# Rotary embedding on half of each head: the first load in two pieces, and one store on another queue

## The chip, the cores and the metric

The kernel runs on one core of one Trainium2 chip. The metric is the device time of one execution in microseconds (us). Runs are repeated, and the median is given with the lowest and the highest. One execution is also taken by the hardware profiler; the profile's times count from the start of its span, which is a little shorter than the time of the execution.

The engines that matter here are VectorE (DVE in the profile), which does all the arithmetic, GpSimd (POOL) and SyncE (SP), which issue transfers, and the core's 16 DMA engines, which carry them. SP's transfers run on the queue that the profile calls q1 (hardware_dynamic), POOL's on q0 (software_dynamic). A trailing q, as in SPq, means an engine's sequencer.

## The reference

```python
batch, seq, heads, dim = (16, 512, 16, 64)          # x is float32
x1, x2 = x[..., :32], x[..., 32:]
cos, sin = cos[None, :, None, :], sin[None, :, None, :]   # given as (512, 32)
first  = x1[..., :16] * cos[..., :16] - x1[..., 16:] * sin[..., :16]
second = x1[..., :16] * sin[..., :16] + x1[..., 16:] * cos[..., :16]
out = concatenate([first, second, x2], axis=-1)
```

The first 32 of each head's 64 numbers are rotated, the other 32 are copied. Only the first 16 columns of cos and sin are used. The input is 33.55 MB and the output as much.

## The kernel before

The input is cut into four tiles (T = 4). A tile has 128 partitions with 16 rows (K) of 1024 floats each, so 64 KB of contiguous memory on each partition and 8.39 MB in all. Half of every row is not changed; the kernel loads it with the rest and stores it from the same place. The tiles live in `ring`, which has three slots (NS = 3), so tile 3 takes the slot of tile 0.

Before the first tile is turned, cos and sin are fetched by GpSimd's queue (lines 63 and 64) into `stage`, after VectorE has cleared it (line 61). VectorE spreads them over the partitions into `table` (lines 73 to 86). Then `rotate(t, lo, hi)` turns the rows lo to hi of a tile in four VectorE instructions: the product with sin goes to the PSUM tile `b_t` (line 96), the product with cos stays in place (line 97), and a subtraction and an addition finish the two halves (lines 98 and 101). A tile is turned in two halves of eight rows (KC = 8), and then stored whole: that is `turn(t)` (line 105).

All loads of x and all stores are issued by SP, in the order in which they are written, and SP waits at each for what it needs. The order is:

- load 0, load 1, the first half of load 2 (lines 65 to 67), which need no wait;
- store 0 (from `turn(0)`), which waits for the rotation of tile 0;
- the second half of load 2 (line 111);
- load 3 in 14 and 2 rows (lines 112 and 113, KL = 14), which needs the slot of tile 0 and so waits for store 0 to land;
- store 1 (line 116), with a wait added by hand (line 115): it is not issued before the first piece of load 3 has landed;
- store 2 and store 3 (lines 121 and 122), each after the rotation of its tile.

The end of the program (line 148 in the profile) waits for all transfers. `load` and `store` are the two helpers at lines 54 and 57, so that all loads have line 55 in the profile, and all stores line 58.

Of the kernel before, what the change touches and what calls it, by code (L numbers as in the profile page):

```python
# [1 line left out]

# [4 lines left out]


@with_exitstack
def kernel(  # L10
    ctx: ExitStack,
    tc: tile.TileContext,
    x: bass.AP,
    cos: bass.AP,
    sin: bass.AP,
    out: bass.AP,
):
    nc = tc.nc
    fp32 = mybir.dt.float32
    P = 128  # L20
    B, S, H, D = x.shape
    Q = D // 4
    HF = D // 2

    K = 16
    T = B * S // (P * K)
    PB = S // K
    REP = P // PB  # L30
    R = H * D
    NS = 3
    KC = K // 2
    KL = 14

    xf = x.rearrange("b s h d -> (b s h d)").rearrange("(t p f) -> t p f", t=T, p=P)
    of = out.rearrange("b s h d -> (b s h d)").rearrange("(t p f) -> t p f", t=T, p=P)
    cosf = cos.rearrange("(p k) j -> p (k j)", k=K)
    sinf = sin.rearrange("(p k) j -> p (k j)", k=K)

    const_pool = ctx.enter_context(tc.tile_pool(name="const", bufs=1))
    b_pool = ctx.enter_context(tc.tile_pool(name="bp", bufs=1, space=bass.MemoryType.PSUM))


    ring = const_pool.tile([P, NS, K, H, D], fp32)
    stage = const_pool.tile([P, 2, K, HF], fp32)
    spun = const_pool.tile([P, 2 * K, Q], fp32)
    packed = const_pool.tile([PB, 2 * K, Q], fp32)
    table = const_pool.tile([P, 2, K, 2, Q], fp32)

    def rows(t, lo, hi):
        return ring[:, t % NS, lo:hi].rearrange("p k h d -> p (k h d)")

    def load(t, lo=0, hi=K):
        return nc.sync.dma_start(out=rows(t, lo, hi), in_=xf[t, :, lo * R : hi * R])

    def store(t, lo=0, hi=K):
        return nc.sync.dma_start(out=of[t, :, lo * R : hi * R], in_=rows(t, lo, hi))


    nc.vector.memset(stage[:, :, :, 0:Q], 0.0)  # L61
    spread = stage.rearrange("(j b) t k i -> j b t (k i)", b=REP)
    nc.gpsimd.dma_start(out=spread[:, 0, 0], in_=cosf)  # L63
    nc.gpsimd.dma_start(out=spread[:, 0, 1], in_=sinf)  # L64
    load(0)
    load(1)
    load(2, 0, KC)

    PQ = PB // REP
    nc.vector.stream_shuffle(  # L73
        out=spun[:],
        in_=stage.rearrange("p t k j -> p (t k) j")[:, :, 0:Q],
        mask=[j % PQ * REP for j in range(PB)],
    )
    for q in reversed(range(REP)):
        n = PQ * (q + 1)
        nc.vector.tensor_copy(out=packed[0:n], in_=spun[q * PB : q * PB + n])  # L80

    for r in range(REP):
        nc.vector.tensor_copy(  # L83
            out=table[r * PB : (r + 1) * PB].rearrange("p t k c j -> p (t k) c j"),
            in_=packed.unsqueeze(2).to_broadcast((PB, 2 * K, 2, Q)),
        )
    C = table[:, 0].rearrange("p k c j -> p k (c j)")
    Sn = table[:, 1].rearrange("p k c j -> p k (c j)")

    def rotate(t, lo, hi):  # L90
        x1 = ring[:, t % NS, lo:hi, :, 0:HF]
        c = C[:, lo:hi].unsqueeze(2).to_broadcast((P, hi - lo, H, HF))
        s = Sn[:, lo:hi].unsqueeze(2).to_broadcast((P, hi - lo, H, HF))
        b_full = b_pool.tile([P, KC, H, HF], fp32, name="b_t")
        b_t = b_full[:, 0 : hi - lo]
        nc.vector.tensor_mul(out=b_t, in0=x1, in1=s)  # L96
        nc.vector.tensor_mul(out=x1, in0=x1, in1=c)  # L97
        nc.vector.tensor_sub(  # L98
            out=x1[:, :, :, 0:Q], in0=x1[:, :, :, 0:Q], in1=b_t[:, :, :, Q:HF]
        )  # L100
        nc.vector.tensor_add(  # L101
            out=x1[:, :, :, Q:HF], in0=x1[:, :, :, Q:HF], in1=b_t[:, :, :, 0:Q]
        )

    def turn(t):
        rotate(t, 0, KC)
        rotate(t, KC, K)
        return store(t)

    turn(0)  # L110
    load(2, KC, K)
    near = load(3, 0, KL)
    load(3, KL, K)

    tc.add_manual_dep(
        turn(1).ins,
        near.ins.name,
        mybir.DependencyInfo(mybir.DependencyClass.Sync, mybir.DependencyReason.DATA),
        reason="the store follows the loads at the DMA engines",
    )  # L120
    turn(2)
    turn(3)


# [1 line left out]
_INS = ['x', 'cos', 'sin']  # L126
_OUTS = [((16, 512, 16, 64), 'float32')]


# [23 lines left out]
```

## Time and profile before

| | us |
|---|---|
| time, median of 4 runs | 161.54 (161.49 to 161.84) |
| time of the profiled execution | 161.56 |
| its span | 159.8 |

The transfers, from their issues and the times to landing in the trace:

| transfer | queue | issued at, us | landed at, us |
|---|---|---|---|
| load 0 (16 rows) | SP | 0.74 | 23.00 |
| load 1 | SP | 1.17 | 42.35 |
| load 2, rows 0 to 8 | SP | 1.64 | 52.07 |
| cos, sin | POOL | 1.70, 2.35 | 10.77, 15.76 |
| store 0 | SP | 49.98 | 71.70 |
| load 2, rows 8 to 16 | SP | 50.37 | 81.42 |
| load 3, rows 0 to 14 | SP | 71.72 | 98.36 |
| load 3, rows 14 to 16 | SP | 72.09 | 100.84 |
| store 1 | SP | 98.43 | 120.16 |
| store 2 | SP | 103.77 | 139.45 |
| store 3 | SP | 130.66 | 158.74 |

VectorE's instructions, by line: eight of each, one per half tile.

| line | tile written <- read | mean, us | first and last start, us |
|---|---|---|---|
| 96 | b_t <- ring, table | 4.433 | 23.1 and 117.2 |
| 97 | ring <- ring, table | 4.424 | 27.6 and 121.7 |
| 98 | ring <- ring, b_t | 2.287 | 32.0 and 126.1 |
| 101 | ring <- ring, b_t | 2.280 | 34.2 and 128.4 |

The first table is read as three views of one time: the median is what counts, the profiled execution is one run, and the span is what its profile covers. In the second table the time between an issue and its landing holds the wait behind earlier transfers on the same queue, so the distance between two landings tells more of a transfer's cost than its own two numbers do. In the profile, a line `SPq L58 <- DVE ring L101` means that SP's sequencer stood before a store (line 58) until VectorE's addition (line 101) was done; the numbers are us in total, times, and the longest. A line of the DMA part gives packets, MB and the share of the time of 16 engines.

### The profile page before, as it was taken

What the parts mean: (1) busy time and instruction counts of PE and PEld (TensorE: products, weight loads), DVE (VectorE), ACT (ScalarE), POOL (GpSimd) and SP (SyncE); (2) the same over time, 40 slices, a digit from 0 to 9 for tenths busy, and PEclk for the clock granted to TensorE, in tenths of its full rate; (3) what the DMA queues carried; (4) which work ended last, traced back from release to release, by engine and by line L of the source; (5) the groups of instructions that cost most, each with busy time, mean ns of one, the idle gap of its engine ahead of it and who ended that gap; (6) DMA issues with size and microseconds to landing.
All of it is one profiled execution on the core that took longest, in us unless ns stands there. A gap on an engine that the chain in (4) does not pass through costs nothing.

```text
span 159.8 us, 113 instructions
## 1 busy us (share of the span) xinstructions
DVE 112.4 (70%) x43; POOL 1.4 (1%) x6
## 2 busy tenths in 40 slices
DVE  1000959999999999999999999999999970000000
POOL 3000000000000000000000000000000000000000
DMA  7969979989699699699999995996996996997993
GB/s 263 525 279 541 459 328 525 410 377 525 287 492 533 295 492 525 263 394 418 500 459 459 459 459 242 546 525 263 525 525 263 525 525 263 525 476 312 525 394 131
DMA packets 1504, 67.24 MB, mean 421 GB/s; under 512 B 192, under 2 KB 192, under 8 KB 224
## 3 DMA queue, kind: packets, MB, share of 16 engines
q1 hardware_dynamic: 1440, 67.11, 97.7%
q0 software_dynamic: 64, 0.13, 0.2%
HBM read 33.69 MB, written 33.55 MB: 421 GB/s over the span
## 4 chain that ended last, share of the span: by engine, by line
DVE 59%; DMA 14%; issue 7%; DVEq 1%
DVE b_t L96 22%; DVE ring L97 22%; DMA ring<-in_x_dram 14%; DVE ring L101 10%; DVE ring L98 4%; DVEq L148 1%; DVEq L96 0%
## 5 line engine op out<-in xcount | busy, mean ns | idle before, releaser
L96 DVE TENSOR_TENSOR b_t<-ring,table 128x4096 f32<-128x4096 f32 x8 | 35.5, 4433 | 2.1 <-DMA ring<-in_x_dram 1.9
L97 DVE TENSOR_TENSOR ring<-ring,table 128x4096 f32<-128x4096 f32 x8 | 35.4, 4424 | 0.3
L98 DVE TENSOR_TENSOR ring<-ring,b_t 128x2048 f32<-128x2048 f32 x8 | 18.3, 2287 | 0.3
L101 DVE TENSOR_TENSOR ring<-ring,b_t 128x2048 f32<-128x2048 f32 x8 | 18.2, 2280 | 0.0
L73 DVE LOAD_MASK_SELECT spun<-stage x1 | 0.0, 14 | 14.5 <-DMA stage<-in_sin_dram 14.5
L83 DVE COPY table<-packed 32x1024 f32<-32x1024 f32 x4 | 2.7, 683 | 0.1
L80 DVE COPY packed<-spun 32x512 f32<-32x512 f32 (+3 forms) x4 | 1.7, 416 | 0.1
L61 DVE MEMSET stage<- 128x512 f32 x1 | 0.5, 485 | 0.9 <-PEq L137 0.9
L73 DVE STREAM_SHUFFLE spun<-stage 128x512 f32<-128x512 f32 x1 | 0.7, 722 | 0.0
L63 POOL DMA_DIRECT2D stage<-in_cos_dram x1 | 0.6, 649 | 1.3 <-DVE stage L61 1.3
L64 POOL DMA_DIRECT2D stage<-in_sin_dram x1 | 0.5, 532 | 0.0
L137 POOL MEMSET const-float32-0.0<- 128x1 f32 x1 | 0.1, 93 | 0.2 <-issue 0.2
L137 POOL MEMSET const-bfloat16-1.0<- 128x1 bf16 x1 | 0.1, 95 | 0.0
L137 POOL MEMSET const-uint8-127<- 128x1 uint8 x1 | 0.1, 93 | 0.0
L137 POOL MEMSET const-float32-1.0<- 128x1 f32 x1 | 0.1, 92 | 0.0
## 6 DMA issues: line engine op xcount, KB each, us to landing
ring<-in_x_dram SPq DMA_DIRECT2D x2, 4096.0 KB, 40.7
ring<-in_x_dram SPq DMA_DIRECT2D x1, 7168.0 KB, 26.6
ring<-in_x_dram SPq DMA_DIRECT2D x1, 1024.0 KB, 28.8
stage<-in_cos_dram POOLq DMA_DIRECT2D x1, 64.0 KB, 9.1
stage<-in_sin_dram POOLq DMA_DIRECT2D x1, 64.0 KB, 13.4
out_dram<-ring SPq DMA_DIRECT2D x4, 24.9
ring<-in_x_dram SPq DMA_DIRECT2D x2, 31.7
```

The source lines that it names most:

```text
L61: nc.vector.memset(stage[:, :, :, 0:Q], 0.0)
L63: nc.gpsimd.dma_start(out=spread[:, 0, 0], in_=cosf)
L64: nc.gpsimd.dma_start(out=spread[:, 0, 1], in_=sinf)
L73: nc.vector.stream_shuffle(out=spun[:], in_=stage.rearrange("p t k j -> p (t k) j")[:, :, 0:Q], mask=[j % PQ * REP for j in range(PB)],)
L80: nc.vector.tensor_copy(out=packed[0:n], in_=spun[q * PB : q * PB + n])
L83: nc.vector.tensor_copy(out=table[r * PB : (r + 1) * PB].rearrange("p t k c j -> p (t k) c j"), in_=packed.unsqueeze(2).to_broadcast((PB, ...
L96: nc.vector.tensor_mul(out=b_t, in0=x1, in1=s)
L97: nc.vector.tensor_mul(out=x1, in0=x1, in1=c)
L98: nc.vector.tensor_sub(out=x1[:, :, :, 0:Q], in0=x1[:, :, :, 0:Q], in1=b_t[:, :, :, Q:HF])
L101: nc.vector.tensor_add(out=x1[:, :, :, Q:HF], in0=x1[:, :, :, Q:HF], in1=b_t[:, :, :, 0:Q])
L137: nc = _bacc.Bacc("TRN2", target_bir_lowering=False, num_devices=1)
L148: with _tile.TileContext(nc) as tc:
```

## The change

Two things are changed. Load 0 is issued as two transfers, rows 0 to 4 (KC // 2 = 4) and rows 4 to 16, in place of one. And `store` and `turn` take a queue, SP's unless another is given; tile 2's is GpSimd's. The rotations and the other transfers are as they were.

```diff
-    def store(t, lo=0, hi=K):
-        return nc.sync.dma_start(out=of[t, :, lo * R : hi * R], in_=rows(t, lo, hi))
+    def store(t, lo=0, hi=K, queue=nc.sync):
+        return queue.dma_start(out=of[t, :, lo * R : hi * R], in_=rows(t, lo, hi))
...
-    load(0)
+    load(0, 0, KC // 2)
+    load(0, KC // 2, K)
     load(1)
     load(2, 0, KC)
...
-    def turn(t):
+    def turn(t, queue=nc.sync):
         rotate(t, 0, KC)
         rotate(t, KC, K)
-        return store(t)
+        return store(t, queue=queue)
...
-    turn(2)
+    turn(2, nc.gpsimd)
     turn(3)
```

## The prediction

> **What bounds the kernel now.** First the page's top: span, busy engines, the row of DMA shares and the queues.
>
> ```profile
> span 159.8 us, 113 instructions
> DVE 112.4 (70%) x43; POOL 1.4 (1%) x6
> ...
> DVE  1000959999999999999999999999999970000000
> ...
> DMA  7969979989699699699999995996996996997993
> ...
> DMA packets 1504, 67.24 MB, mean 421 GB/s; under 512 B 192, under 2 KB 192, under 8 KB 224
> q1 hardware_dynamic: 1440, 67.11, 97.7%
> q0 software_dynamic: 64, 0.13, 0.2%
> ```
>
> VectorE is idle in the first tenth and the last sixth; the DMA engines are busy from end to end. (A slice under 9 is not idle: a packet's bytes are counted where it starts.) Then the packets of one queue in a stretch that holds nothing but store 1 and store 2:
>
> ```profile
> DMA packets 112, 7.34 MB, mean 432 GB/s; under 512 B 0, under 2 KB 0, under 8 KB 0
> q1 hardware_dynamic: 112, 7.34, 99.6%
> ```
>
> 112 packets in 17 us (101 to 118) are 65,536 B each; sixteen engines busy 99.6% make 16 x 17 x 0.996 / 112 = 2.419 us a packet. The packet records say 2.418 us, and by size: 57,344 B 2.116, 32,768 B 1.213, 8,192 B 0.309, 4,096 B 0.159, a semaphore write 0.009. All lie on bytes / 27.2 GB/s plus 0.0085 us, so a transfer cut finer pays 0.0085 us per extra packet and engine. Third, the waits of SP's queue, and the end of the chain:
>
> ```profile
> SPq L58 <- DVE ring L101: 58.3, 3, 26.9
> SPq L58 <- DMA ring<-in_x_dram: 46.8, 2, 25.8
> SPq L148 <- DMA out_dram<-ring: 27.7, 1, 27.7
> ```
>
> ```profile
> 128.43 2.20 DVEq L148
> ```
>
> The page's chain says 59% DVE and stops at 130.6 us, with the last compute instruction. What comes after is the third wait: SP sits 27.7 us until store 3 lands (158.74). That is DMA time. Store 3 is issued at 130.66, while store 2 still runs until 139.45; store 3 lands 19.29 us later, eight packets of 2.418 (19.34). So no stall of VectorE, POOL or SP under 8 us in the store phase reaches the end. From first packet (1.75) to last (158.3) each engine adds up to its bytes with three excesses: about 0.6 us on the first packet, about 0.6 us where store 0 gives way to load 2's second half (68 to 72 us), and 0.8 us of packet overhead.
>
> **The change part by part.** The sum starts from the profiled execution: 161.56 us, of which 159.78 is the span and 1.78 lies around it. The median of the runs is 161.54, so the two can be taken as one.
>
> *Load 0 in two.* One SP issue more (rows of L55: 0.33 to 0.43 us). It pushes load 1's issue from 1.17 to about 1.6 and load 2's first half from 1.64 to about 2.1; their packets are wanted at 22 and 41 us, so nothing is late, and what covers it is some 20 us of load 0. Per engine there are 8 packets more (16 instead of 8) and one semaphore write: 8 x 0.0085 + 0.009 = **+0.08 us**. All DMA is one saturated stream, so this is paid in full at the end.
>
> What it doesn't buy is an earlier start. The first rotation takes rows 0 to 8 (KC = 8) and the cut is at row 4, so it needs both pieces, and the second lands where load 0 landed, 23.0 us, plus 0.08. What does come earlier is cos and sin:
>
> ```profile
> q1 hardware_dynamic: 128, 8.39, 98.4%
> q0 software_dynamic: 64, 0.13, 1.7%
> issues: line engine op xcount, KB each, median us to landing
> ring<-in_x_dram SPq DMA_DIRECT2D x1, 4096.0 KB, 50.4
> stage<-in_cos_dram POOLq DMA_DIRECT2D x1, 64.0 KB, 9.1
> stage<-in_sin_dram POOLq DMA_DIRECT2D x1, 64.0 KB, 13.4
> ```
>
> In this stretch (1.7 to 22 us) q0 gets one packet after each q1 packet, and four such turns of 2.4 us make sin land at 15.8. With 16 KB rows (2.418 / 4 = 0.61 us) the turns are short: sin about 7 to 9 us, the table about 13 instead of 21.25. VectorE then waits for load 0 as it does now, only longer:
>
> ```profile
> DVE spun L73 <- DMA stage<-in_sin_dram: 14.5, 1, 14.5
> DVE b_t L96 <- DMA ring<-in_x_dram: 1.9, 1, 1.9
> ```
>
> The 1.9 is the slack of the table today; earlier cos and sin fall wholly into it: 0.
>
> Store 0 is issued 26.98 us after load 0 lands, and load 1 with load 2a occupy the engines for 29 us after it, so store 0 arrives as these run out (issue 49.98, first packet 51.06, and no gap in the records). Both ends of that move with load 0's landing, so the fit stays.
>
> *Start-up.* The first packets take 2.62 to 3.38 us instead of 2.42, an excess of about 0.6. No row shows a first packet of 16 KB. If the excess is a latency, it stays (0); if it grows with the packet, three quarters go (-0.5). The nearest row is the turn from store 0 to a load with 32 KB packets: 0.6 too, at half the size. That speaks for a latency: 0, range -0.5 to 0.
>
> *Store 2 on POOL's queue.* SP loses one issue of 0.343 us (103.77) and a semaphore wait; store 3 was behind it, but waits for VectorE until 130.63, so that is worth 0. POOL gets a wait on VectorE's rotation of tile 2 (103.74 us) with nothing behind it but the end of the program, and an issue. The rows are 0.649 and 0.532 us for 32 rows of 2 KB; for 128 rows between 0.5 and 4 x 0.65 = 2.6 us. That lies beside store 1, whose packets last until 120 us. Without that cover it would be paid in full.
>
> At the engines store 2 then alternates with store 1 packet by packet from about 106 on, instead of following it. The bytes are the same: store 1 should land near 130 instead of 120.2, store 2 near 145 instead of 139.5, store 3 where it did. The price of the software queue's packets is open from both sides. Its only data packets here are 4,096 B (0.13 MB in 32), 0.159 us, on the line of the others, and a q1 packet follows one with no gap. If a 64 KB row is one packet, the price is 0; if it is cut into 4,096 B packets, 128 x 0.159 - 8 x 2.418 = **+1.0 us**. The 4 KB packets here are two whole rows together, and a row of any size on q1 is one packet; the nearest reading is a row left whole: 0, range 0 to +1.0. A gain has no room, since q1 alone already fills 99.6%. At the end SP waits on one semaphore more: 0.06 us between its last waits, 0 to +0.06.
>
> The Trainium skill, "SBUF — State Buffer", section "SBUF: two separate sides", speaks against this edit: it says that GpSimd cannot write descriptors while VectorE runs a two-port performance-mode instruction, so that a DMA issued from GpSimd stalls behind VectorE. Here VectorE works without a break from 23.10 to 130.6 us, and cos and sin were issued before that, so no row of this trace shows the case. "VectorE: DVE Perf Modes", section "Mode 2×_2P — use both read ports for one tensor", says that tensor_tensor can't run in that mode, and tensor_tensor is all that runs here; by that page the cost is 0, by the first page's stall it is the second rival below.
>
> Sum: 161.56 + 0.08 + 0 + 0 = 161.64, or **161.6 us**: no change. A difference under 0.2% (0.32 us) can't be told from none in this kernel.
>
> **The rivals.**
>
> 1. *Small packets on the software queue*, slower: store 2 in pieces of about 4 KB, or a loss at each turn between the queues of like size. For it: the 4,096 B packets. Against: the reading above. Paid in full since nothing is idle: 161.64 + 1.0 = 162.6 us.
>
> 2. *POOL starved by VectorE*, slower. The gaps between VectorE's instructions are 0.02 us. If POOL can't write its descriptors until VectorE stops at 130.63, store 1 runs out at 120.2 and the engines idle until about 131.7 (1.0 us from issue to packet, as at the start: 0.74 to 1.75). Then stores 2 and 3 take 16 x 2.418 = 38.7: landing 170.8 instead of 158.74, so 161.6 + 12.0 = 173.6 us. It decides only once POOL's start slips beyond 118 us, 14 us after its wait ends, longer than a whole rotation of half a tile (4.43 + 4.42 + 2.29 + 2.28 = 13.4 us); a shorter stall is hidden by store 1.
>
> 3. *Cheaper start-up*, faster: the first packet's excess shrinks with the packet, 161.64 - 0.5 = 161.1 us. Against it: the turn at 70 us.
>
> 4. *The split does start VectorE earlier.* It can't: rows 4 to 7 are in the second piece. And if it did, store 0 would only queue behind loads that already fill the engines until 51 us. It gives 161.6 too and is counted there.
>
> **How the numbers follow.** No change 0.55, rival 1 0.21, rival 2 0.07, rival 3 0.17. The predicted time is 161.6, its own range 161.4 to 161.8. The full range goes from rival 3 (161.0) past rival 1 (162.6), to 162.8; outside are rival 2 and some scatter. Faster 0.17, same 0.55, slower 0.28.
>
> **What would show it.** Right: sin landing before 10 us and the first L96 still starting at about 23.1; the wait L96 <- load grown from 1.9 to about 10 us; q0 with 8.5 MB in few packets (about 64 + 144); stores 1 and 2 alternating with no idle slice between 106 and 131; store 3 landing at 158.8. Rival 1 shows as over 1,000 packets more, rival 2 as idle DMA slices from 120 to 131 us, rival 3 as load 0 landing before 22.7. The forecast is wrong if the mean GB/s between 106 and 145 falls below 430, or if VectorE's first L96 moves.

## The result and the profile after

| | before | after |
|---|---|---|
| median, us | 161.53 (55 runs) | 161.67 (34 runs) |
| lowest to highest, us | 161.31 to 161.84 | 161.31 to 163.57 |
| runs above 161.9 us | 0 | 15 |
| the profiled execution, us | 161.56 | 161.63 |
| its span, us | 159.8 | 159.8 |

The ratio is 1.0026, with a 95% interval of [1.0014, 1.0038]. The two medians are 0.09% apart, inside the 0.2% that counts as no change; the ratio says a quarter of a per cent slower, because the changed kernel has two kinds of executions. 19 of 34 lie from 161.31 to 161.70, where the kernel before lies, and 15 from 161.9 to 163.6, where it never does. The profile shows one of the first kind, so it can't show the loss. Its top, in the same parts of the page as before:

```profile
span 159.8 us, 115 instructions
DVE 112.4 (70%) x43; POOL 1.9 (1%) x7
...
DVE  1048029999999999999999999999999960000000
...
DMA  5999999989699699699999996996996996996990
...
DMA packets 1648, 67.24 MB, mean 421 GB/s; under 512 B 208, under 2 KB 208, under 8 KB 240
q1 hardware_dynamic: 1440, 58.72, 85.6%
q0 software_dynamic: 208, 8.52, 12.3%
```

8.39 MB have gone from q1 to q0, and q0 has 144 packets more (208 for 64): 128 rows of 64 KB, one packet each, and 16 semaphore writes. The engines are as full as before.

The waits of VectorE, of POOL and of SP (us in total, times, longest):

```profile
DVE spun L74 <- DMA stage<-in_sin_dram: 8.6, 1, 8.6
DVE b_t L97 <- DMA ring<-in_x_dram: 7.5, 1, 7.5
```

```profile
POOL out_dram L58 <- DVE ring L102: 101.0, 1, 101.0
```

```profile
SPq L58 <- DVE ring L102: 56.6, 2, 29.6
SPq L58 <- DMA ring<-in_x_dram: 47.7, 3, 25.5
SPq L149 <- DMA out_dram<-ring: 27.9, 1, 27.9
```

sin is there 6 us earlier (14.5 has become 8.6), and VectorE spends nearly all of it waiting for load 0 (1.9 has become 7.5). The last wait, for store 3, is about as long as it was (27.9 for 27.7). The store phase, 104 to 131 us, by queue:

```profile
DMA packets 176, 11.53 MB, mean 427 GB/s; under 512 B 0, under 2 KB 0, under 8 KB 0
q1 hardware_dynamic: 96, 6.29, 53.7%
q0 software_dynamic: 80, 5.24, 44.8%
```

Six packets of store 1 and five of store 2 on each engine, in turn, 98.5% of the time taken. Store 1 lands at 132.20 (before 120.16), store 2 at 144.26 (139.45), store 3 at 158.72 (158.74).

### The profile page after: what moved, and what is told of

Read it like the earlier page. It is cut to its first block, busy times and chain, and to the rows that moved or that the text cites. A ratio compares the mean times of both kernels' runs of the same rounds, so it can differ in the third digit from the quotient of the medians.

```text
span 159.8 us, 115 instructions
## 1 busy us (share of the span) xinstructions
DVE 112.4 (70%) x43; POOL 1.9 (1%) x7
## 4 chain that ended last, share of the span: by engine, by line
DVE 59%; DMA 14%; issue 7%; DVEq 1%; SPq 0%
DVE b_t L97 22%; DVE ring L98 22%; DMA ring<-in_x_dram 14%; DVE ring L102 10%; DVE ring L99 4%; DVEq L149 1%; SPq L55 0%; DVEq L97 0%
## 5 line engine op out<-in xcount | busy, mean ns | idle before, releaser
L97 DVE TENSOR_TENSOR b_t<-ring,table 128x4096 f32<-128x4096 f32 x8 | 35.5, 4433 | 7.8 <-DMA ring<-in_x_dram 7.5
L58 POOL DMA_DIRECT2D out_dram<-ring x1 | 0.6, 559 | 101.0 <-DVE ring L102 101.0
```

Source lines behind the costliest of these rows:

```text
L58: return queue.dma_start(out=of[t, :, lo * R : hi * R], in_=rows(t, lo, hi))
```

## The experiments

Twelve kernels were run, each against the kernel before on the same chip. "4 and 12 rows" is the split of the changed kernel, `load(0, 0, KC // 2); load(0, KC // 2, K)`. early1 and early3 leave a part of tile 0's rotation out, so that their output is not the reference's; the edits are shown below.

| run | load 0 | store 2 on | median, us | lowest to highest | above 161.9 | ratio, interval |
|---|---|---|---|---|---|---|
| again | 4 and 12 rows | POOL | 162.03 | 161.38 to 162.99 | 6 of 12 | 1.0033 [1.0012, 1.0054] |
| split_only | 4 and 12 rows | SP | 161.65 | 161.36 to 162.99 | 5 of 12 | 1.0028 [1.0006, 1.0050] |
| pool_only | whole | POOL | 161.62 | 161.46 to 161.76 | 0 of 11 | 1.0004 [0.9995, 1.0012] |
| act_store | 4 and 12 rows | ScalarE | 161.86 | 161.40 to 163.09 | 5 of 11 | 1.0030 [1.0008, 1.0053] |
| rot4 | 4 and 12 rows | SP | 162.56 | 162.45 to 162.69 | 5 of 5 | 1.0062 [1.0049, 1.0074] |
| halves | 8 and 8 rows | SP | 162.68 | 162.59 to 162.82 | 5 of 5 | 1.0070 [1.0058, 1.0083] |
| split_late | 4 and 12 rows | SP | 163.03 | 162.61 to 163.20 | 5 of 5 | 1.0081 [1.0067, 1.0095] |
| late | whole | SP | 161.71 | 161.54 to 161.89 | 0 of 11 | 1.0008 [0.9999, 1.0017] |
| split_load1 | whole (load 1 in 4 and 12) | SP | 161.62 | 161.49 to 162.29 | 2 of 11 | 1.0010 [1.0001, 1.0019] |
| early1 | whole | SP | 161.34 | 161.20 to 161.78 | 0 of 11 | 0.9991 [0.9982, 1.0000] |
| early3 | whole | SP | 161.40 | 161.33 to 161.66 | 0 of 11 | 0.9993 [0.9984, 1.0002] |
| split_early | 4, 11.5 and 0.5 rows | SP | 161.67 | 161.50 to 162.59 | 3 of 11 | 1.0020 [1.0004, 1.0036] |

### Which of the two edits

Four kernels: the changed one again, each edit alone, and the changed one with ScalarE's queue in place of POOL's. The theories have letters: Q says that the late executions (those above 161.9 us) come from the second queue, S that they come from the small first rows of the split.

```diff
# split_only, against the changed kernel
-    turn(2, nc.gpsimd)
+    turn(2)
# pool_only
-    load(0, 0, KC // 2)
-    load(0, KC // 2, K)
+    load(0)
# act_store
-    turn(2, nc.gpsimd)
+    turn(2, nc.scalar)
```

> The changed kernel once more, for its scatter: 19 of its 34 executions lay between 161.31 and 161.70 us, as the kernel before does, and 15 between 161.9 and 163.6. Both theories expect the same here: some 40% of the executions above 161.9, the rest at 161.4. If it shows no execution above 161.9, the scatter belongs to the chip on which it ran and not to the kernel.

> Load 0 in 4 and 12 rows, all stores on SP. Theory Q (the late executions come from the software queue beside SP's): no execution above 161.9, median 161.4 to 161.6. Theory S (they come from the small first rows at the start, which leave the 16 DMA engines or the store behind them out of step): some 40% above 161.9, up to 163.5.

> Load 0 whole, tile 2's store on GpSimd's queue. Theory Q: some 40% of the executions above 161.9, up to 163.5. Theory S: none above 161.9, median 161.5.

> As the changed kernel, but tile 2's store goes to ScalarE's queue, a second hardware queue beside SP's. Theory Q in the form that software makes the difference: the late executions go away unless they come from the split. Theory Q in the form that two queues side by side make it: they stay, some 40% above 161.9. Theory S: they stay too, and split_only tells these two apart.

The scatter is the kernel's (again, 6 of 12), and it follows the split: 5 of 12 with the split alone, 0 of 11 with POOL's queue alone. With ScalarE's queue it is 5 of 11, no fewer than without a second queue, so theory Q falls in both forms. The store on POOL's queue is worth nothing, 1.0004 with an interval that holds 1.

act_store's profile caught one of the late executions (162.50 us). Until 103 us SP's queue carries the same transfers there as in the changed kernel, so its waits can be laid beside those shown above:

```profile
SPq L58 <- DMA ring<-in_x_dram: 48.8, 3, 26.5
SPq L149 <- DMA out_dram<-ring: 28.7, 1, 28.7
```

Store 1's wait for load 3 is 1.0 us longer (26.5 for 25.5), and so is nearly the wait for the last store (28.7 for 27.9). The transfer ahead of them is the second half of load 2, seen here in a window that holds its issue (KB, us from issue to landing):

```profile
ring<-in_x_dram SPq DMA_DIRECT2D x1, 4096.0 KB, 32.0
```

The same line in the changed kernel's profile:

```profile
ring<-in_x_dram SPq DMA_DIRECT2D x1, 4096.0 KB, 31.2
```

Each transfer's 16 completions, one per DMA engine, say more: 14 engines have this load finished by 81.31 us, the other two at 81.83 and 82.29 (in the changed kernel's profile all 16 lie from 81.00 to 81.36). It shows first where store 0 ends: 14 completions of store 0 lie by 71.59, the other two at 71.72 and 71.89. Load 3's first piece is complete by 98.25 on 14 engines, and at 98.78 and 99.24 on two, so store 1, which waits for the last of them, is issued at 99.32 (98.39 in the changed kernel). Two are still behind at the end: store 3 is complete by 158.85 on 14 engines (by 158.72 on all 16 in the changed kernel), and at 159.13 and 159.60 on the last two. The loss of this execution begins on two engines, where store 0 gives way to load 2, and most of it stays there.

### Store 0 against the end of the loads

The next theory, J, was that store 0 reaches the engines just as the loads run out, and that the split upsets this. Four kernels: store 0 issued 6 us earlier with the split kept (rot4); store 0 later without the split (late); one more transfer, not at the start (split_load1); other first rows (halves).

```diff
# rot4: the split, and
-    turn(0)
+    rotate(0, 0, KC // 2)
+    rotate(0, KC // 2, KC)
+    rotate(0, KC, K)
+    store(0)
# late, against the kernel before
-    turn(0)
+    rotate(0, 0, KC)
+    nc.vector.tensor_mul(out=spun[:, 0:28], in0=spun[:, 0:28], in1=spun[:, 0:28])
+    rotate(0, KC, K)
+    store(0)
# split_load1, against the kernel before
-    load(1)
+    load(1, 0, KC // 2)
+    load(1, KC // 2, K)
# halves, against the kernel before
-    load(0)
+    load(0, 0, KC)
+    load(0, KC, K)
```

> Load 0 in 4 and 12 rows as in split_only, and tile 0 rotated in 4, 4 and 8 rows, so that VectorE starts at about 15.5 us and store 0 is issued some 6 us earlier (43 to 44 instead of 49.8). Theory J (store 0 reaches the DMA engines just as their loads run out; the split lets some engines run dry before it, and the late executions come from that): no execution above 161.9, median 161.4 to 161.5. Theory S (the 16 KB rows at the start leave the engines out of step, whatever store 0 does): some 40% above 161.9 as in split_only. Theory N (one more transfer ahead of the turn from store 0 to load 2): the same 40%.

> The kernel before with one VectorE product more of about 0.5 us between the two rotations of tile 0 (on a scratch tile, the output is the same), so that store 0 is issued at about 50.5 and not 49.98. Theory J: the engines run dry for up to half a us, late executions appear, or all are later by 0.4 or more (161.9 to 163). Theories S and N: within 0.5 us of before, 161.5 to 162.0, and no scatter.

> The kernel before with load 1 instead of load 0 in 4 and 12 rows: the start is as before, the number of transfers as in the changed kernel. Theory N: some 40% of the executions above 161.9. Theories S and J: none, median 161.5 to 161.6.

> Load 0 in 8 and 8 rows: the first rotation needs the first piece alone, so VectorE starts when the table is ready and store 0 is issued 5 to 7 us earlier; the start has rows of 32 KB. Theory J: no execution above 161.9, median 161.4 to 161.6. Theory S: scatter stays, perhaps in fewer executions. Theory N: some 40% above 161.9.

No theory had foreseen rot4 and halves: both about 1 us later than before, in every run. late was a miss: the product was scheduled ahead of the first rotation, into the time in which VectorE waits for load 0, and store 0 was issued at 49.87, as usual. split_load1 has 2 runs of 11 above 161.9 (161.91 and 162.29).

Where rot4 loses is seen in one stretch, 46 to 53 us. It holds the same 96 packets in the three kernels; what differs is the share of the engines' time that they take. The kernel before:

```profile
DMA packets 96, 3.15 MB, mean 449 GB/s; under 512 B 16, under 2 KB 16, under 8 KB 16
q1 hardware_dynamic: 96, 3.15, 104.0%
```

The changed kernel:

```profile
q1 hardware_dynamic: 96, 3.15, 104.1%
```

And rot4, where store 0 was issued at 43.35 and not at 49.8:

```profile
q1 hardware_dynamic: 96, 3.15, 120.4%
```

The share is over 100% because whole packets are counted where they start. The difference, 16.4% of 7 us, is 1.15 us on each engine, for the same bytes. These are load 2's last packets: with store 0 queued behind them long before, they take up to 2.3 us and not 1.21. At the next turn, from store 0 to load 2's second half, rot4 pays nothing where the kernel before pays 0.53 us, so that 0.62 us are left, of the 0.8 us by which its span is longer (160.6 for 159.8).

So the profiles were read for two turns: the last loads before store 0 (46 to 53 us), and store 0 to the second half of load 2 (66 to 76 us). The table has the time that packets took beyond bytes / 27.2 GB/s plus 0.0085 us, summed from the packet records and divided by 16 engines. The lead is the time from store 0's issue to the end of the loads ahead of it (the mean end, over the 16 engines, of their last packets before store 0); the rows are in its order.

| profile of | store 0 issued, us | lead, us | excess at 46 to 53, us | excess at 66 to 76, us |
|---|---|---|---|---|
| rot4 | 43.35 | 9.02 | 1.15 | 0.00 |
| halves | 44.02 | 8.40 | 1.12 | 0.00 |
| early3 | 49.00 | 2.40 | 0.08 | 0.07 |
| split_early | 49.26 | 2.06 | 0.01 | 0.18 |
| the changed kernel | 49.79 | 1.91 | 0.01 | 0.06 |
| early1 | 49.46 | 1.80 | 0.01 | 0.16 |
| split_load1 | 49.77 | 1.76 | 0.18 | 0.13 |
| again | 49.72 | 1.54 | 0.09 | 0.28 |
| split_only | 49.81 | 1.42 | 0.01 | 0.42 |
| late | 49.87 | 1.39 | 0.00 | 0.45 |
| act_store | 49.87 | 1.37 | 0.01 | 0.59 |
| before | 49.98 | 1.31 | 0.00 | 0.53 |
| pool_only | 50.13 | 1.12 | 0.01 | 0.66 |
| split_late | 50.46 | 0.79 | 0.06 | 0.99 |

By the time of issue alone the changed kernel and split_load1 would not fit. Their loads end later, at 51.70 and 51.53 us (51.23 to 51.39 in the other ten with an issue from 49.0 us on): the changed kernel's profile has 0.47 us of excess within load 1, split_load1's 0.12 us more than before at the start and 0.18 at the first turn. Why they have it is open. By the lead they stand where the others do. Most of the second excess is on store 0's own last packets, which start near 68 us (in the kernel before they take up to 3.36 us and not 2.418).

### Store 0 earlier or later by a little

Before early1, early3, split_late and split_early had been run, the rows of the table that were there led to theory K: a store that is queued too early costs, and the split brings it too early.

```diff
# split_late: the split, and
-    turn(0)
+    rotate(0, 0, KC)
+    rotate(0, KC, KC + KC // 2)
+    rotate(0, KC + KC // 2, K)
+    store(0)
# early1, against the kernel before (early3: H - 3)
-        nc.vector.tensor_mul(out=x1, in0=x1, in1=c)
+        w = H - 1 if (t, lo) == (0, KC) else H
+        nc.vector.tensor_mul(out=x1[:, :, 0:w], in0=x1[:, :, 0:w], in1=c[:, :, 0:w])
```

> Load 0 in 4 and 12 rows, all stores on SP, and tile 0's second half rotated in two pieces of 4 rows, which costs VectorE about 0.64 us more (four instructions more) and puts store 0 at 50.4 instead of 49.8. Theory K (what decides is when store 0 is issued against the last load packets, which start at 49.8 to 50.5: a store that is queued before an engine has begun its last load packet costs that engine about 1.2 us at the turn from loads to stores, as on all engines of rot4 and halves; one that comes just after costs nothing there): no execution above 161.9, median 161.4 to 161.7. Theory S (the 16 KB rows at the start): 40% above 161.9.

> The kernel before with one of 16 heads left out of the product with cos in rows 8 to 16 of tile 0, which takes 0.27 us off VectorE and puts store 0 at 49.7, where the split has it. Load 0 is whole. Theory K: late executions appear without any split, some 20 to 60% above 161.9. Theory S: none, median 161.5.

> The same with three heads left out, 0.80 us off VectorE, store 0 at 49.2. Theory K: most executions above 161.9, median 162 to 162.7, towards the 162.6 of rot4 and halves, and the profile shows the excess in the last load packets at 48 to 51 us. Theory S: none above 161.9, median 161.5.

Theory K falls on all three. A store issued 0.5 to 1.0 us earlier (49.46 and 49.00 for 49.98) costs nothing and may gain a little (0.9991 and 0.9993, both intervals reaching to 1); with one issued 0.65 us later than in split_only the median is 1.4 us above split_only's (163.03 for 161.65), and all five executions are late. In split_late's profile the engines stand idle at 51 us, 0.17 us on the mean of the 16, and the turn at 66 to 76 costs 0.99 instead of 0.4 to 0.6. Its engines also end further apart: store 3's 16 completions are spread over 0.97 us (0.43 in split_only). SP's longest wait for a load shows the later turn, 26.4 us where split_only has 25.8. In split_late:

```profile
SPq L58 <- DMA ring<-in_x_dram: 46.6, 2, 26.4
```

In split_only:

```profile
SPq L58 <- DMA ring<-in_x_dram: 45.9, 2, 25.8
```

Together with the table: between a lead of 1.8 and one of 0.8 us, every us by which store 0 comes later against the end of the loads goes with some 0.8 us more of excess at the next turn ((0.99 - 0.16) / (1.80 - 0.79)); from 1.8 to 2.4 us it stays at 0.06 to 0.18, and at the leads of 8 and 9 us the cost is at the first turn. Between 2.4 and 8 us no kernel was run. The kernel before, with 1.31, sits on that slope. These are single profiles; what makes the packets longer is not shown.

What remained was whether the split's scatter comes from that slope. The last kernel keeps the 4 rows at the start, cuts off half a row at the end of load 0, and so starts the rotation and store 0 earlier, at 49.26:

```diff
# split_early, against the kernel before
-    load(0)
+    flat = rows(0, 0, K)
+    cuts = (0, KC // 2 * R, K * R - R // 2, K * R)
+    for a, z in zip(cuts, cuts[1:]):
+        nc.sync.dma_start(out=flat[:, a:z], in_=xf[0, :, a:z])
```

> Load 0 in three pieces: rows 0 to 4 as in the changed kernel, then up to the middle of row 15, then the last half row. The first rotation (rows 0 to 8) needs the first two alone and starts about 0.6 us earlier than in split_only, so that store 0 is issued at about 49.2; all stores on SP, the output is the reference's. Theory J2 (store 0 comes too late by a few tenths of a us: the issue time read off the profiles so far goes with the excess at the turn from store 0 to load 2, 49.0 with 0.08 us, 49.5 with 0.17, 49.8 with 0.44, 50.0 with 0.55, 50.1 with 0.69, 50.5 with 1.07, and the split's late executions are those in which single engines meet it later still): no execution above 161.9, median 161.3 to 161.5, excess at that turn about 0.1. Theory S (the 16 KB rows at the start scatter the engines, whatever store 0 does): some 40% above 161.9, as in split_only.

The mean excess fell about as expected (0.18 at 66 to 76, with a lead of 2.06). The late executions stayed, 3 of 11 (162.37, 162.43, 162.59). Theory J2 falls as the cause of the scatter; 3 of 11 beside 5 of 12 doesn't say whether an earlier store makes it rarer. Theory S is what is left, and it is a place rather than a mechanism. It isn't shown in the form in which it was stated either, "whatever store 0 does": rot4 has the same first rows, and its five executions lie within 0.24 us of each other. At split_only's rate of 5 late ones in 12, five in a row without the scatter have a chance of some 7%.

## Why the prediction was right, and where it was not

The time was right: 161.6 forecast, median 161.67, the single profiles nearly equal. The kernel is "no change" by its median, and slower by 0.26% [0.14, 0.38] by the ratio, which no step of the sum held. That the median came so near has luck in it: with nearly half of the executions late (31 of 69 in the changed kernel, again, split_only and act_store), the median falls in the one group or the other, and again, the same kernel, had 162.03.

*Store 2 on POOL's queue: 0, range 0 to +1.0.* Right, and shown alone by pool_only (1.0004). Each row was left whole (128 packets of 65,536 B, 2.418 us each), which ends the first rival. POOL's issue beside VectorE at work:

```profile
103.58 4.43 DVE L97 TENSOR_TENSOR b_t<-ring,table 128x4096 f32<-128x4096 f32 x1
103.84 0.56 POOL L58 DMA_DIRECT2D out_dram<-ring  x1 [100.97 <-DVE ring L102]
```

0.56 us, near the 0.53 and 0.64 of cos and sin, in the middle of a VectorE instruction: not starved, so the second rival is out too. Store 2's first packets start at 109.68 and not at about 106, after two more of store 1's on each engine; on ScalarE's queue (act_store, issued at 103.65) it is the same on 14 of the 16 engines, so that delay is not POOL's. From 106 to 145 us the engines moved 430 GB/s, as before. The stall of which the Trainium skill warns, "SBUF — State Buffer", section "SBUF: two separate sides", did not show beside tensor_tensor, which by its page "VectorE: DVE Perf Modes", section "Mode 2×_2P — use both read ports for one tensor", can't run in the two-port mode that the warning is about. Its page "DMA: Bandwidth & Descriptors", section "Issuing engines are not separate DMA queues", says that DMAs of all issuing engines run on the same DMA engines and interleave; here, with the split, store 2 on POOL's queue gave ratios of 1.0026 and 1.0033, on ScalarE's 1.0030 and on SP's 1.0028.

*Load 0 in two: +0.08 us, paid in full.* This is the term that was mis-sized. Its packets are as costed (16 KB 0.611 us, 48 KB 1.815 us), but that is not what the split costs: alone it measured 1.0028 [1.0006, 1.0050], and not as a shift of all runs (the 19 faster runs of the changed kernel have a median of 161.43, below the 161.53 of the kernel before) but as a second group of runs, 0.4 to 2 us later, in some 45% of them. "Paid in full at the end" does not hold ahead of store 0 either: the changed kernel's profile lost 0.47 us within load 1, paid 0.06 and not 0.53 at the turn behind store 0, and has the span of the kernel before.

*"Store 0 arrives as these run out ... so the fit stays."* The arrival was read rightly, but the price was taken as nothing on either side. split_late and rot4 show it, though both have the split as well: issued 0.65 us later than in split_only, the kernel is 1.4 us slower; issued 6 us earlier, with the full work, it is 1.0 us slower than the kernel before. The absence of an idle slice at 51 us was no proof that store 0 came in time: a lead under some 1.8 us goes with longer packets 17 us later.

*"The turn at 70 us ... speaks for a latency", against the third rival.* Right end, wrong reason. The turn's 0.6 us is no fixed latency, it goes from 0.06 to 0.99 with store 0's lead. That the start got no cheaper is shown by the first packets themselves: 0.55 us of excess per engine in the changed kernel and 0.49 to 0.62 in the other kernels with the 4 and 12 rows, 0.55 to 0.75 where load 0 is whole.

*The split starts nothing earlier.* Right: the first L97 begins at 22.90 (before 23.10; 22.85 to 23.25 in the other profiles with load 0 whole). The wait for load 0 grew to 7.5 us and not to about 10, because the table was done at 15.4 and not at 13: 15 of sin's 16 completions lie by 8.43 us, the last, behind a 48 KB packet, at 9.90.

What stays open is why single DMA engines fall behind in some executions once load 0 is split. Of these executions one was profiled; there it happened where store 0 gives way to load 2, on two of 16 engines. The scatter is not the second queue's, and not that of the mean lateness of store 0. Whether it is the small first rows or one more transfer ahead of that turn isn't settled: split_load1, which has the second without the first, gave 2 of 11, on another chip than split_only. Kernels that leave the rotation incomplete (early1, early3) were the only ones below the kernel before; one that issues store 0 half a us earlier with load 0 whole and the full work was not run.

## What to carry to other kernels

Where the DMA engines are the bound, look at the turns between loads and stores: in this kernel the lead with which a store was queued there had a price on both sides, even where no engine showed an idle slice. Take the spread of many runs before calling an edit neutral: the profile and the lower half of the runs of this kernel are those of the kernel before, and the loss is in the other half. And an earlier transfer of part of a tile is worth something only if the first instruction that reads the tile can do with that part.

## What the runs showed that had not been expected

- With a store issued 8 to 9 us before the loads ahead of it ended, the last load packets took 1.12 to 1.15 us more per DMA engine (rot4 and halves; 120.4% for 104.0% in rot4); with 0.8 to 2.4 us, 0.00 to 0.18 us. In return the next turn, from the store to a load, was free (0.00 for 0.53 us).
- From a lead of 1.8 us down to 1.1 us the store leaves no gap at its own place, but an excess that grows from 0.16 to 0.66 us at the turn after it; at 0.8 us it is 0.99 us, with 0.17 us of idle time at the store's own place.
- A loss ahead of the store can come back at the turn behind it: 0.47 us within load 1 in the changed kernel's profile, then 0.06 for 0.53 us at the turn, and the span is the same (159.8 us).
- In a late execution 2 of 16 DMA engines ended a load 0.5 and 1.0 us behind the others and were still 0.28 and 0.75 us behind at the end of the program (159.13 and 159.60 us, the others by 158.85).
- A software-queue packet of 65,536 B takes as long as a hardware-queue one (2.418 us), and the two queues take turns packet by packet with no gap.
